# Small fp32 products of a mixer's branches: one by one between dense steps, or in runs

## The chip, the core and the metric

The kernel runs on one core of one Trainium2 chip. Its time is the device time of one launch in microseconds (us); of several runs the median is given. Five engines work in parallel, each through its own queue in order: TensorE (PE in the profile, its weight loads PEld), VectorE (DVE), ScalarE (ACT), GpSimd (POOL) and SyncE (SP), which issues most of the DMAs. They wait for each other through semaphores.

## The reference

One layer of a trunk on 512 tokens of width 1024: a mixer of four branches, cross attention to 256 memory tokens, and a gated feed-forward network with a convolution. Each is normed before and after, all in fp32. What matters here are three of the four branches:

```python
def gla_branch(q, k, v, r, a_lr, w_alpha, b_alpha, norm_g):      # chunks of 64 tokens, 4 heads of 64
    glog = jax.nn.log_sigmoid((a_lr @ w_alpha + b_alpha)) / GLA_TAU     # a_lr has 16 columns
    gcum = jnp.cumsum(heads(glog), axis=2)
    ...
    scores = jnp.where(causal, jnp.einsum('bnihd,bnjhd->bnhij', q_dec, k_dec), 0.0)
    o_intra = jnp.einsum('bnhij,bnjhv->bnihv', scores, vh)
    kv = jnp.einsum('bnjhd,bnjhv->bnhdv', k_to_end, vh)
    # a scan over the 8 chunks: state = exp(decay) * state + kv
    o = o_intra + jnp.einsum('bnihd,bnhdv->bnihv', q_dec, s_prev)
    o = o * lax.rsqrt(jnp.mean(o * o, axis=-1, keepdims=True) + EPS)
    return o * norm_g * jax.nn.silu(r)

def sgu_branch(u, v, ln_g, ln_b, w_s, b_s):                      # chunks of 128 tokens, 4 groups of 64
    vn = layer_norm(v, ln_g, ln_b)
    mixed = jnp.einsum('gij,bnjgc->bnigc', w_s * mask, vn) + b_s
    return u * mixed

def rglru_branch(xr, gate, ...):                                 # a linear recurrence over the tokens
    xc = causal_dwconv(xr, conv_w, conv_b)
    r, i = sigmoid(xc @ w_a + b_a), sigmoid(xc @ w_x + b_x)      # block-diagonal, 4 blocks of 64
    ...
```

## The kernel before

All activations are kept channel-major: a tile holds 128 channels by 512 tokens. The large products ("dense") are computed from fp32 values that are split into a high and a low part (type fp32r), as three products each: high by high, low by high and high by low (lines 125, 126 and 127, the function `mm3`). One such triple for one 128-row block of the contraction is a k-step, and `dense` makes eight of them for a contraction over 1024. The input projections (`w_in`, tile `win`) are eighteen dense products in a row, each with its own 128 output channels; then come the gates (tile `gate`) and the products of the branches with `w_branch` (tile `br`), 8 + 2 k-steps for each of 8 output blocks and 4 branches. Weights come by DMA into `raw`, ScalarE casts them to `whi` (line 75), and VectorE subtracts for `wlo` (line 76).

The branches' own small products are plain fp32, which TensorE does in two passes (two matmul rows in the profile for each). They are written as generators, called fibers. After each k-step `dense` calls `pump()`, which advances the first fiber to its next `yield`. So what a fiber issues between two yields stands between two k-steps of TensorE, up to what the tile framework's scheduler moves in ordering each engine's queue.

- `decay_fiber` issues the rank-16 product z (line 406, 16 rows of the array, four products), from which ScalarE and VectorE make the decays (tile `ee`, then `m`, `e`, `ep` and `dl`). `sgu_fiber` makes the layer norm (`vn`) and the token mixing `mx` (line 383, sixteen products, 64 columns of the array each, a pair on the two halves of the columns between two yields). Both run beside the first two projections, whose outputs are taken from PSUM by `kr` (line 352, VectorE).
- `gla_fiber(p)`, once for each half p of the heads, issues four transposes `ktT` (line 432, copied by ScalarE to `ktt`), eight score products `s` (line 442, 64 rows of the array each, first four on the one half hh of the rows, then four on the other), seven state products `kv` (line 457, 64 rows each, alternating halves), and for the output `o` eight products with 64 columns each (line 477) and seven on the whole array (line 482). VectorE masks the scores into `st` (line 446) and makes the running states `ss` (lines 468 and 470), two instructions per chunk. Then come a norm over heads (`hsum`, line 490, `rw`, `rbg`, line 501).
- `lru_fiber(p)` issues `gr` and `gi` (line 551, whole array).

PSUM has eight banks, which are allotted in turn: two with tag A (the outputs of the dense projections and gates), four with tag B (`ktT`, `s`, `kv`, `o`) and two with tag C (`z`, `mx`, `gr`, `gi`, `hsum`, `rbg`, `br`).

Of the kernel before, what the change touches and what calls it, by code (L numbers as in the profile page):

```python
# [16 lines left out]
P = 128  # L17
# [22 lines left out]
def tile_trunk(ctx: ExitStack, tc: tile.TileContext, a: dict, out: bass.AP):  # L40
# [114 lines left out]
            put(src)  # L155
        return hi, lo

# [1 line left out]
    par = cp.tile([P, NPAR], F32, name="par")  # L159

    def pc(name, i):
# [61 lines left out]
                              start=True, stop=True)  # L223
        return ps

# [1 line left out]
    x = [get(f"x{k}") for k in range(KT)]  # L227
    VA = 256 + 16
    vps = [bank("B", f"va{t}") for t in range(4)]
# [76 lines left out]
    def vtok(t, c0, c1):  # L306
        return vt[t // 2][:, (t % 2) * 256 + c0:(t % 2) * 256 + c1]

# [1 line left out]
    lngb = get("lngb")  # L310
    sync.dma_start(lngb[:, 0:256], a["ln_g"].partition_broadcast(P))
    sync.dma_start(lngb[:, 256:512], a["ln_b"].partition_broadcast(P))
# [30 lines left out]
    R2 = range(2)  # L343
# [8 lines left out]
        vector.tensor_tensor(t, ps, rb0s, op=ALU.mult)  # L352
        return t

# [1 line left out]
    mixed = []  # L356

    def sgu_fiber():
        vn = []
        for t in range(4):  # L360
            if t % 2 == 0:
                vnt = get("vn")
                vn.append(vnt)
            c = slice((t % 2) * 256, (t % 2 + 1) * 256)
            sv = svt[t // 2][:, c]
            st6 = tp.tile([P, 6], F32, tag="st6", name=f"st6_{t}")
            vector.bn_stats(st6, sv)
            mv = tp.tile([P, 2], F32, tag="mv", name=f"mv_{t}")
            vector.bn_aggr(mv, st6)
            sd = tp.tile([P, 1], F32, tag="sd", name=f"sd_{t}")  # L370
            scalar.activation(sd, mv[:, 1:2], AF.Sqrt, bias=epsc)
            vector.reciprocal(sd, sd)
            vector.tensor_scalar(vnt[:, c], sv, mv[:, 0:1], sd, op0=ALU.subtract, op1=ALU.mult)
            vector.tensor_mul(vnt[:, c], vnt[:, c], lngb[:, 0:256])
            vector.tensor_add(vnt[:, c], vnt[:, c], lngb[:, 256:512])
            yield
        put(*svt, lngb)
        for p in R2:
            mx = bank("C", "mx")
            for t in range(4):  # L380
                for j in R2:
                    g = 2 * p + j
                    tensor.matmul(mx[j * 64:(j + 1) * 64, t * P:(t + 1) * P],
                                  lhsT=vn[t // 2][:, (t % 2) * 256 + g * 64:(t % 2) * 256 + (g + 1) * 64],
                                  rhs=sguw[:, g * P:(g + 1) * P], start=True, stop=True)
                yield
            yc = get("yc")
            vector.tensor_tensor(yc.rearrange("p (n i) -> p n i", n=4), mx.rearrange("p (n i) -> p n i", n=4),
                                 sgub[:, p * P:(p + 1) * P].unsqueeze(1).to_broadcast([P, 4, P]), op=ALU.add)
            vector.tensor_mul(yc, yc, rb0s)  # L390
            mixed.append(yc)
        put(*vn, sguw, sgub)

# [1 line left out]
    gl_q = [get("ep") for _ in R2]  # L395
    gl_k = [get("e") for _ in R2]
    gl_kte = [get("m") for _ in R2]
# [3 lines left out]
    def decay_fiber():  # L401
        zs = [bank("C", "z") for _ in R2]
        for p in R2:
            for t in R2:
                tt = slice(t * 256, (t + 1) * 256)
                tensor.matmul(zs[p][:, tt], lhsT=walpha[:, p * P:(p + 1) * P], rhs=alr[0:16, tt],
                              start=True, stop=True)
                yield
        ee = wp.tile([P, 1024], F32, tag="raw", bufs=4, name="ee")
        for p in R2:  # L410
            scalar.activation(ee[:, p * S:(p + 1) * S], zs[p], AF.Abs, bias=pc("balpha", p))
            vector.tensor_scalar(gl_kte[p], zs[p], pc("balpha", p), 0.0, op0=ALU.add, op1=ALU.min)
        scalar.activation(ee, ee, AF.Exp, scale=-1.0)
        scalar.activation(ee, ee, AF.Ln, bias=1.0)
        for p in R2:
            vector.tensor_sub(gl_kte[p], gl_kte[p], ee[:, p * S:(p + 1) * S])
            vector.tensor_tensor_scan(gl_k[p], scanm, gl_kte[p], 0.0, op0=ALU.mult, op1=ALU.add)
        for p in R2:
            gc3 = gl_k[p].rearrange("p (n i) -> p n i", i=64)
            last = gc3[:, :, 63:64]  # L420
            vector.tensor_sub(gl_kte[p].rearrange("p (n i) -> p n i", i=64), last.to_broadcast([P, 8, 64]), gc3)
            scalar.activation(gl_dl[p].unsqueeze(2), last, AF.Exp, scale=1.0 / 16.0)
            scalar.activation(gl_q[p], gl_k[p], AF.Exp, scale=1.0 / 16.0)
            scalar.activation(gl_kte[p], gl_kte[p], AF.Exp, scale=1.0 / 16.0)
            scalar.activation(gl_k[p], gl_k[p], AF.Exp, scale=-1.0 / 16.0)
            vector.tensor_mul(gl_q[p], gl_q[p], rb0s)
        put(alr, scanm)

    def gla_fiber(p):
        kt_ps = bank("B", "ktT")  # L430
        for t in range(4):
            tensor.transpose(kt_ps[:, t * P:(t + 1) * P], gl_kte[p][:, t * P:(t + 1) * P], ident)
            yield
        ktt = get("ktt")
        scalar.copy(ktt, kt_ps)
        st = []
        for hh in R2:
            f = slice(hh * 64, hh * 64 + 64)
            s_ps = bank("B", "s")
            for t in range(4):  # L440
                tt = slice(t * P, (t + 1) * P)
                tensor.matmul(s_ps[:, tt], lhsT=gl_k[p][f, tt], rhs=gl_q[p][f, tt], start=True, stop=True)
                yield
            sm = get("st")
            gpsimd.memset(sm, 0.0)
            vector.copy_predicated(sm.rearrange("p (n i) -> p n i", n=4),
                                   causal.bitcast(I32).unsqueeze(1).to_broadcast([P, 4, P]),
                                   s_ps.rearrange("p (n i) -> p n i", n=4))
            st.append(sm)
        ss = [get("ss") for _ in R2]  # L450
        for t in ss:
            gpsimd.memset(t, 0.0)
        kv = [bank("B", "kv0"), bank("B", "kv1")]
        for n in range(7):
            r = slice((n % 2) * 64, (n % 2) * 64 + 64)
            c = slice((n // 2) * P, (n // 2 + 1) * P)
            tensor.matmul(kv[n % 2][:, c], lhsT=ktt[r, c], rhs=vtok(n // 2, p * P, (p + 1) * P)[r, :],
                          start=True, stop=True)
            yield
            for hh in R2:  # L460
                f = slice(hh * 64, hh * 64 + 64)

                def at(m):
                    return ss[m // 4][f, (m % 4) * P + hh * 64:(m % 4) * P + hh * 64 + 64]

                src = kv[n % 2][f, (n // 2) * P + hh * 64:(n // 2) * P + hh * 64 + 64]
                if n == 0:
                    vector.tensor_copy(at(1), src)
                else:
                    vector.scalar_tensor_tensor(at(n + 1), at(n), gl_dl[p][f, n:n + 1], src,  # L470
                                                op0=ALU.mult, op1=ALU.add)
        o_ps = bank("B", "o")
        for t in range(4):
            tt = slice(t * P, (t + 1) * P)
            for hh in R2:
                f = slice(hh * 64, hh * 64 + 64)
                tensor.matmul(o_ps[f, tt], lhsT=vtok(t, p * P + hh * 64, p * P + hh * 64 + 64),
                              rhs=st[hh][:, tt], start=True, stop=False)
            yield
            for n in (2 * t, 2 * t + 1):  # L480
                if n > 0:
                    tensor.matmul(o_ps[:, n * 64:(n + 1) * 64], lhsT=ss[n // 4][:, (n % 4) * P:(n % 4 + 1) * P],
                                  rhs=gl_q[p][:, n * 64:(n + 1) * 64], start=False, stop=n % 2 == 1)
            yield
        sq = get("sq")
        scalar.activation(sq, o_ps, AF.Square)
        yield
# [11 lines left out]
        for t in range(4):  # L499
            tt = slice(t * P, (t + 1) * P)  # L500
            tensor.matmul(rb[:, tt], lhsT=rw[:, tt], rhs=ident, start=True, stop=True)
            yield
        scalar.copy(sq, rb)
        vector.scalar_tensor_tensor(sq, o_ps, pc("glang", p), sq, op0=ALU.mult, op1=ALU.mult)
        put(*st, ktt, *ss, rw, gl_q[p], gl_k[p], gl_kte[p])
# [3 lines left out]
        put(gl_r[p])  # L509
        y[1][p] = split(sq, "yb", True)  # L510

# [1 line left out]
    lam = cp.tile([P, 2], F32, name="lam")  # L513
    la = [tp.tile([P, 2], F32, tag=f"la{i}", bufs=1, name=f"la{i}") for i in range(5)]
    pos8, neg8 = la[3], la[4]
# [27 lines left out]
    def lru_fiber(p, rx):  # L543
# [4 lines left out]
        for i, ps in enumerate((gr, gi)):  # L548
            for t in R2:
                tt = slice(t * 256, (t + 1) * 256)  # L550
                tensor.matmul(ps[:, tt], lhsT=lruw[:, i * 256 + p * P:i * 256 + (p + 1) * P], rhs=xc[:, tt],
                              start=True, stop=True)
                yield
        rr, ii = rx, get("ii")
        scalar.activation(rr, gr, AF.Sigmoid, bias=pc("lba", p))
        scalar.activation(ii, gi, AF.Sigmoid, bias=pc("lbx", p))
# [14 lines left out]
        put(rr)  # L571
        y[3][p] = split(gg, "yd", True)

# [1 line left out]
    fibers += [decay_fiber(), sgu_fiber()]  # L575
    for p in R2:
        kr = normed(w_in(), "kr")
# [41 lines left out]
        put(r)  # L619
        gl_r.append(sg)  # L620

# [1 line left out]
    acc = [None] * KT  # L623
    merged = []
    for ki, kb in enumerate(order):
# [23 lines left out]
        put(*t)  # L649
    put(rb0s, lruw, *vt)  # L650

# [1 line left out]
    mm = [get("mem") for _ in range(4)]  # L653
    for j in range(4):
        sync.dma_start(mm[j], a["memT"][j])
# [25 lines left out]
        if m == KT - 3:  # L681
            scalar.activation(warm, yg[m][:, tok][:, 0:1], AF.Sqrt, scale=0.0, bias=epsc)

# [1 line left out]
    yg, ssum = [], {}  # L685
    for m in range(KT):
        ps = bank("A", "mo")
# [30 lines left out]
            h2.append(split(hk, "h2", True))  # L718
        return h2

# [1 line left out]
    kk = [(get("kh", F32R), get("kl", F32R)) for _ in range(4)]  # L722
    for m in range(KT):
        ps = bank("A", "kT")
# [19 lines left out]
    for t in mem:  # L744
        put(*t)

# [1 line left out]
    def wq(hd):  # L748
        q = []
        for i in range(2):  # L750
# [127 lines left out]
    for c, ts in kept:  # L878
        put(*ts)

# [1 line left out]
    def up_post(j, ps):  # L882
        u = get("u")
        vector.tensor_tensor(u, ps, rb3, op=ALU.mult)
# [174 lines left out]
```

## Time and profile before

| what | value |
|---|---|
| three runs | 979.79, 980.82, 980.82 us, median 980.82 |
| profiled execution: span from its first to its last instruction | 978.7 us (its own launch time is not among the data; the median run is 2.1 us above this span) |
| TensorE busy, weight loads busy | 964.3 us, 802.6 us |
| VectorE busy, ScalarE busy | 574.7 us, 420.7 us |
| granted clock of TensorE, mean | 0.996 |
| first z to last rbg (the stretch of the small products) | 34 to 196 us |

The timeline gives the start of an instruction, its duration, engine, line, operation, tiles written and read, the shape, and how many alike were put together (x2). Matmuls are pipelined and the next starts before the last one's row ends, so what an instruction costs is read from the starts of what follows it. The groups by line give count, busy time and mean ns. A bracket at the end of a row is the idle time of that engine before it, and who ended it.

### The profile page before, as it was taken

How to read it: one execution, taken by the hardware profiler on the slowest of the kernel's cores; microseconds unless marked ns; L12 is line 12 of the kernel's file. 1: busy time of each engine (PE TensorE's matmuls, PEld its weight loads, DVE VectorE, ACT ScalarE, POOL GpSimd, SP SyncE). 2: the span in 40 equal slices, each digit the busy share in tenths (PEclk: the TensorE clock that was granted, in tenths of full speed). 3: DMA queues.
4: the chain of work that ended last, by engine and by line, in shares of the span. 5: the costliest groups of instructions: out<-in, count | busy, mean ns of one | idle time of the engine just before them, and what ended most of it. 6: DMA issues, size and time to landing. Idle time of an engine off the chain costs nothing.

```text
span 978.7 us, 12151 instructions
## 1 busy us (share of the span) xinstructions
PE 964.3 (99%) x4782; PEld 802.6 (82%) x4782; DVE 574.7 (59%) x886; ACT 420.7 (43%) x637; POOL 11.8 (1%) x33
## 2 busy tenths in 40 slices
PE   7999999999999999999999999999999999999996
PEld 7778687688888888889888889988888888888886
DVE  4776456445455565639865635897777777622314
ACT  7836136233223353545644554554444444322411
POOL 2000000000000000000000000000000000000001
PEclk9999999999999999999999999999999999999998
DMA  9342122132334333335431340132323232332302
GB/s 333 120 126 88 44 86 64 47 105 89 106 103 134 119 97 107 108 96 163 151 113 60 108 130 1 63 106 91 105 89 106 88 104 85 96 96 86 116 1 86
DMA packets 32648, 98.27 MB, mean 100 GB/s; under 512 B 4288, under 2 KB 7248, under 8 KB 32592
## 3 DMA queue, kind: packets, MB, share of 16 engines
q1 hardware_dynamic: 32416, 97.48, 31.4%
q8 instruction: 37, 0.61, 0.3%
q14 instruction: 19, 0.16, 0.1%
q0 software_dynamic: 32, 0.02, 0.0%
q10 hardware_dynamic: 144, 0.00, 0.0%
HBM read 95.39 MB, written 2.10 MB: 100 GB/s over the span
## 4 chain that ended last, share of the span: by engine, by line
PE 97%; issue 1%; ACT 1%; DVE 0%; DMA 0%; SPq 0%; DVEq 0%
PE up L126 8%; PE up L125 8%; PE up L127 8%; PE gate L125 6%; PE gate L127 6%; PE gate L126 6%; PE dn L127 4%; PE dn L125 4%; PE dn L126 4%; PE win L125 4%; PE win L127 3%; PE win L126 3%; PE br L125 2%; PE wo L127 2%; PE wo L125 2%; PE wo L126 2%
## 5 line engine op out<-in xcount | busy, mean ns | idle before, releaser
L75 ACT CAST whi<-raw 128x1024 fp32r<-128x1024 f32 x158 | 164.4, 1042 | 316.3 <-issue 146.0
L76 DVE TENSOR_TENSOR wlo<-raw,whi 128x1024 fp32r<-128x1024 f32 x158 | 191.1, 1211 | 129.9 <-ACT whi L75 128.5
L127 PE MATMUL up<-h3h,wlo 128*128 128x512 f32 (+1 forms) x368 | 138.2, 376 | 0.0
L126 PE MATMUL up<-h3l,whi 128*128 128x512 f32 (+1 forms) x368 | 138.1, 375 | 0.0
L125 PE MATMUL up<-h3h,whi 128*128 128x512 f32 (+1 forms) x368 | 138.1, 375 | 0.0
L125 PE MATMUL gate<-xgh,whi 128*128 128x512 f32 x256 | 101.9, 398 | 0.0
L127 PE MATMUL gate<-xgh,wlo 128*128 128x512 f32 x256 | 100.0, 390 | 0.0
L126 PE MATMUL gate<-xgl,whi 128*128 128x512 f32 x256 | 99.7, 389 | 0.0
L127 PEld LDWEIGHTS up<-h3h,wlo 128*128 128x128 f32 x368 | 69.3, 188 | 12.6
L125 PEld LDWEIGHTS up<-h3h,whi 128*128 128x128 f32 x368 | 69.3, 188 | 12.5
L126 PEld LDWEIGHTS up<-h3l,whi 128*128 128x128 f32 x368 | 69.3, 188 | 12.2
L352 DVE TENSOR_TENSOR sg<-gate,rb0s 128x512 f32<-128x512 f32 x32 | 22.1, 690 | 81.5 <-PE gate L127 81.5
L538 DVE SCALAR_TENSOR_TENSOR c<-u,par,c 128x511 f32<-128x511 f32 (+1 forms) x88 | 65.0, 746 | 1.3
L125 PE MATMUL win<-xgh,whi 128*128 128x512 f32 x144 | 61.0, 424 | 0.0
L125 PE MATMUL dn<-gh,whi 128*128 128x512 f32 x154 | 59.9, 389 | 0.0
L126 PE MATMUL dn<-gl,whi 128*128 128x512 f32 x154 | 59.9, 389 | 0.0
L127 PE MATMUL dn<-gh,wlo 128*128 128x512 f32 x154 | 59.9, 389 | 0.0
L125 PEld LDWEIGHTS gate<-xgh,whi 128*128 128x128 f32 x256 | 48.1, 188 | 11.4 <-issue 0.5
L127 PE MATMUL win<-xgh,wlo 128*128 128x512 f32 x144 | 56.6, 393 | 0.0
L127 PEld LDWEIGHTS gate<-xgh,wlo 128*128 128x128 f32 x256 | 48.1, 188 | 10.2
L126 PE MATMUL win<-xgl,whi 128*128 128x512 f32 x144 | 56.3, 391 | 0.0
L126 PEld LDWEIGHTS gate<-xgl,whi 128*128 128x128 f32 x256 | 48.1, 188 | 8.9
(348 smaller groups left out, 1752.5 us busy)
## 6 DMA issues: line engine op xcount, KB each, us to landing
raw<-in_w_up SPq DMA_DIRECT2D x44, 512.0 KB, 3.5
raw<-in_w_gate SPq DMA_DIRECT2D x32, 512.0 KB, 3.5
raw<-in_w_in SPq DMA_DIRECT2D x18, 512.0 KB, 3.5
raw<-in_w_down SPq DMA_DIRECT2D x16, 512.0 KB, 3.6
raw<-in_w_br SPq DMA_DIRECT2D x8, 512.0 KB, 3.4
raw<-in_w_mix SPq DMA_DIRECT2D x8, 512.0 KB, 3.5
raw<-in_w_k SPq DMA_DIRECT2D x8, 512.0 KB, 3.5
raw<-in_w_v SPq DMA_DIRECT2D x8, 512.0 KB, 3.5
```

Source lines behind the costliest of these rows:

```text
L75: scalar.copy(hi[:, :n], raw[:, :n])
L76: vector.tensor_tensor(lo[:, :n], raw[:, :n], hi[:, :n].bitcast(F32), op=ALU.subtract)
L125: tensor.matmul(ps, lhsT=w[0], rhs=x[0], start=first, stop=False)
L126: tensor.matmul(ps, lhsT=w[0], rhs=x[1], start=False, stop=False)
L127: tensor.matmul(ps, lhsT=w[1], rhs=x[0], start=False, stop=last)
L352: vector.tensor_tensor(t, ps, rb0s, op=ALU.mult)
L538: vector.scalar_tensor_tensor(dst[:, s:S], src[:, 0:S - s], pc(wname, (taps - 1 - s) * stride + off), dst[:, s:S], op0=ALU.mult, op1=ALU.add)
```

## The change

The yields are moved. z's four products, mx's sixteen, ktT's four with s's eight, kv's seven, o's fifteen, gr and gi's four and rbg's four are each issued between two k-steps. The eight products of s alternate between the halves of the rows, which write two banks. The state updates now come after all kv products, one chunk per yield. In front of mx and of kv the fiber passes three k-steps. In o only the first product on each half of the columns clears the bank (`start`), and the products with the states come after all others. The number of products, their operands and their shapes stay. Comments that fall away shift nothing; line numbers after the changed places move by a few (442 becomes 444, 457 becomes 463, 383 becomes 385).

```diff
@@ sgu_fiber
         put(*svt, lngb)
+        for _ in range(3):
+            yield
+        mxs = [bank("C", "mx") for _ in R2]
         for p in R2:
-            mx = bank("C", "mx")
             for t in range(4):
                 for j in R2:
                     g = 2 * p + j
-                    tensor.matmul(mx[j * 64:(j + 1) * 64, t * P:(t + 1) * P],
+                    tensor.matmul(mxs[p][j * 64:(j + 1) * 64, t * P:(t + 1) * P],
                                   ...
-                yield
+        yield
+        for p in R2:
+            mx = mxs[p]
             yc = get("yc")
...
@@ decay_fiber
                 tensor.matmul(zs[p][:, tt], lhsT=walpha[:, p * P:(p + 1) * P], rhs=alr[0:16, tt],
                               start=True, stop=True)
-                yield
+        yield
...
@@ gla_fiber
             tensor.transpose(kt_ps[:, t * P:(t + 1) * P], gl_kte[p][:, t * P:(t + 1) * P], ident)
-            yield
         ktt = get("ktt")
         scalar.copy(ktt, kt_ps)
+        sps2 = [bank("B", f"s{hh}") for hh in R2]
+        for t in range(4):
+            tt = slice(t * P, (t + 1) * P)
+            for hh in R2:
+                f = slice(hh * 64, hh * 64 + 64)
+                tensor.matmul(sps2[hh][:, tt], lhsT=gl_k[p][f, tt], rhs=gl_q[p][f, tt], start=True, stop=True)
+        yield
         st = []
         for hh in R2:
-            f = slice(hh * 64, hh * 64 + 64)
-            s_ps = bank("B", "s")
-            for t in range(4):
-                tt = slice(t * P, (t + 1) * P)
-                tensor.matmul(s_ps[:, tt], lhsT=gl_k[p][f, tt], rhs=gl_q[p][f, tt], start=True, stop=True)
-                yield
             sm = get("st")
             ...
+        for _ in range(3):
+            yield
         kv = [bank("B", "kv0"), bank("B", "kv1")]
         for n in range(7):
             ...
             tensor.matmul(kv[n % 2][:, c], lhsT=ktt[r, c], rhs=vtok(n // 2, p * P, (p + 1) * P)[r, :],
                           start=True, stop=True)
-            yield
+        yield
+        for n in range(7):
             for hh in R2:
                 ...
                     vector.scalar_tensor_tensor(at(n + 1), at(n), gl_dl[p][f, n:n + 1], src,
                                                 op0=ALU.mult, op1=ALU.add)
+            yield
         o_ps = bank("B", "o")
         for t in range(4):
             ...
                 tensor.matmul(o_ps[f, tt], lhsT=vtok(t, p * P + hh * 64, p * P + hh * 64 + 64),
-                              rhs=st[hh][:, tt], start=True, stop=False)
-            yield
-            for n in (2 * t, 2 * t + 1):
-                if n > 0:
-                    tensor.matmul(o_ps[:, n * 64:(n + 1) * 64], lhsT=ss[n // 4][:, (n % 4) * P:(n % 4 + 1) * P],
-                                  rhs=gl_q[p][:, n * 64:(n + 1) * 64], start=False, stop=n % 2 == 1)
-            yield
+                              rhs=st[hh][:, tt], start=t == 0, stop=False, skip_group_check=True)
+        for n in range(1, 8):
+            tensor.matmul(o_ps[:, n * 64:(n + 1) * 64], lhsT=ss[n // 4][:, (n % 4) * P:(n % 4 + 1) * P],
+                          rhs=gl_q[p][:, n * 64:(n + 1) * 64], start=False, stop=n == 7, skip_group_check=True)
+        yield
...
             tensor.matmul(rb[:, tt], lhsT=rw[:, tt], rhs=ident, start=True, stop=True)
-            yield
+        yield
...
@@ lru_fiber
                 tensor.matmul(ps[:, tt], lhsT=lruw[:, i * 256 + p * P:i * 256 + (p + 1) * P], rhs=xc[:, tt],
                               start=True, stop=True)
-                yield
+        yield
```

TensorE at the scores of the first half of the heads, beside the projection `win_973` (names carry the number of the tile; `xgh` and `xgl` are the parts of the activations). Before:

```order
L127 MATMUL win_973<-xgh_278,wlo_906 128x512
L442 MATMUL s_1010<-ep_514,e_516 128x128
L125 MATMUL win_973<-xgh_312,whi_905 128x512
L126 MATMUL win_973<-xgl_313,whi_905 128x512
L127 MATMUL win_973<-xgh_312,wlo_906 128x512
L442 MATMUL s_1010<-ep_514,e_516 128x128
L125 MATMUL win_973<-xgh_351,whi_905 128x512
```

After, where the two names `s_117_998` and `s_118_999` are the two banks:

```order
L127 MATMUL win_973<-xgh_140,wlo_906 128x512
L436 MATMUL ktT_991<-ident,m_518 128x128 x4
L444 MATMUL s_117_998<-ep_514,e_516 128x128
L444 MATMUL s_118_999<-ep_514,e_516 128x128
L444 MATMUL s_117_998<-ep_514,e_516 128x128
L444 MATMUL s_118_999<-ep_514,e_516 128x128
L444 MATMUL s_117_998<-ep_514,e_516 128x128
L444 MATMUL s_118_999<-ep_514,e_516 128x128
L444 MATMUL s_117_998<-ep_514,e_516 128x128
L444 MATMUL s_118_999<-ep_514,e_516 128x128
L125 MATMUL win_973<-xgh_171,whi_905 128x512
```

The products of the first head's half stood behind one k-step each; all eight now stand behind the transposes, without a k-step between them.

VectorE at the end of the second projection, whose bank `kr` empties (`yc` is the mixed tokens of the spatial gating). Before:

```order
L388 TENSOR_TENSOR yc_662<-mx_641,sgub_494 128x512
L352 TENSOR_TENSOR kr_678<-win_618,rb0s_394 128x512
L390 TENSOR_TENSOR yc_662<-yc_662,rb0s_394 128x512
L578 TENSOR_TENSOR m_519<-kr_678,m_519 128x512
L579 TENSOR_TENSOR e_517<-kr_678,e_517 128x512
```

After:

```order
L392 TENSOR_TENSOR yc_662<-mx_641,sgub_494 128x512
L392 TENSOR_TENSOR yc_665<-mx_642,sgub_494 128x512
L394 TENSOR_TENSOR yc_662<-yc_662,rb0s_394 128x512
L394 TENSOR_TENSOR yc_665<-yc_665,rb0s_394 128x512
L352 TENSOR_TENSOR kr_683<-win_628,rb0s_394 128x512
```

Three of the four `yc` instructions that stood behind `kr` or around it are now ahead of it.

VectorE at the states of the second half of the heads (`ydl` and `gg` belong to the recurrence, `sg` to the gates). Before:

```order
L153 TENSOR_TENSOR ydl_1405<-gg_1020,ydh_1404 128x512
L468 COPY ss_1500<-kv_183_1504 64x64 x2
L470 SCALAR_TENSOR_TENSOR ss_1500<-ss_1500,dl_521,kv_184_1505 64x64 x2
L470 SCALAR_TENSOR_TENSOR ss_1500<-ss_1500,dl_521,kv_183_1504 64x64 x2
L470 SCALAR_TENSOR_TENSOR ss_1501<-ss_1500,dl_521,kv_184_1505 64x64 x2
L470 SCALAR_TENSOR_TENSOR ss_1501<-ss_1501,dl_521,kv_183_1504 64x64 x2
```

After:

```order
L477 SCALAR_TENSOR_TENSOR ss_1428<-ss_1428,dl_521,kv_180_1460 64x64
L571 SCALAR_TENSOR_TENSOR rx_865<-av_1386,xc_1365 128x512
L477 SCALAR_TENSOR_TENSOR ss_1428<-ss_1428,dl_521,kv_180_1460 64x64
L576 TENSOR_TENSOR gg_1049<-gg_1049,rx_865 128x512
L477 SCALAR_TENSOR_TENSOR ss_1428<-ss_1428,dl_521,kv_179_1459 64x64 x2
L477 SCALAR_TENSOR_TENSOR ss_1429<-ss_1428,dl_521,kv_180_1460 64x64
L153 TENSOR_TENSOR ydl_1396<-gg_1049,ydh_1395 128x512
```

The states came behind the recurrence; they now stand among its scan (`rx`, line 571) and what follows it. On ScalarE in the same place, the copy `ktt` now stands ahead of the cast `whi` and of the sigmoid `sg` that it stood behind. The other engines' queues keep their instructions, and SyncE its DMAs.

More of the change, by code (lines that the diff above doesn't have):

```diff
@@ L447, in gla_fiber @@
                                    causal.bitcast(I32).unsqueeze(1).to_broadcast([P, 4, P]),
-                                   s_ps.rearrange("p (n i) -> p n i", n=4))
+                                   sps2[hh].rearrange("p (n i) -> p n i", n=4))
             st.append(sm)
```

## Prediction

> **What bounds the kernel now.** I read the page first: span, engines, granted clock, chain; then what TensorE waits for.
>
> ```profile
> span 978.7 us, 12151 instructions
> ...
> PE 964.3 (99%) x4782; PEld 802.6 (82%) x4782; DVE 574.7 (59%) x886; ACT 420.7 (43%) x637; POOL 11.8 (1%) x33
> ...
> PEclk9999999999999999999999999999999999999998
> ...
> PE 97%; issue 1%; ACT 1%; DVE 0%; DMA 0%; SPq 0%; DVEq 0%
> ```
> ```profile
> PE va L239 <- ACT xgh L253: 4.5, 1, 4.5
> ```
>
> The chain of waits is TensorE almost throughout, at a steady full clock, and its longest wait for another engine is 4.5 us in the first norm, before anything that changes. So whatever TensorE spends less between 34 and 196 us shortens the program, unless it then waits for someone. TensorE's busy share does not tell the cost of a small product, because matmuls overlap; the distance between the starts of dense steps does. That is read in the timeline of TensorE, an undisturbed step first, then steps with one small product behind them:
>
> ```profile
> 57.50 0.39 PE L125 MATMUL win<-xgh,whi 128*128 128x512 f32 x1
> ...
> 58.18 0.39 PE L125 MATMUL win<-xgh,whi 128*128 128x512 f32 x1
> ```
> ```profile
> 97.28 0.50 PE L125 MATMUL win<-xgh,whi 128*128 128x512 f32 x1
> ...
> 98.17 0.48 PE L442 MATMUL s<-ep,e 64*128 64x128 f32 x2
> 98.59 0.50 PE L125 MATMUL win<-xgh,whi 128*128 128x512 f32 x1
> ...
> 111.71 0.51 PE L125 MATMUL win<-xgh,whi 128*128 128x512 f32 x1
> ...
> 113.02 0.50 PE L125 MATMUL win<-xgh,whi 128*128 128x512 f32 x1
> ```
>
> A plain step lasts 58.18 - 57.50 = 0.68. With a score product s (98.59 - 97.28) or a state product kv (113.02 - 111.71) it lasts 1.31: each costs 0.63. What is product and what is excursion, full-array products in a run tell:
>
> ```profile
> 26.26 1.05 PE L221 MATMUL bctok<-ident,rs 128*128 128x128 f32 x8
> 27.07 0.36 PE L239 MATMUL sv<-svwh,xgh 128*128 128x256 f32 x1
> ```
>
> Eight passes (an fp32 product is two) of 128 moving columns take 0.81, so a pass takes 0.10 to 0.11 and a product 0.21. Of the 0.63, 0.42 goes into leaving the full array and coming back.
>
> **Part by part.** How many there are:
>
> ```profile
> L442 PE MATMUL s<-ep,e 64*128 64x128 f32 x32 | 7.8, 322 | 0.0
> L457 PE MATMUL kv<-vt,ktt 64*128 64x128 f32 x28 | 6.8, 322 | 0.0
> ```
>
> 32 and 28 passes are 16 and 14 products; 15 a fiber, 15 x 0.63 = 9.45. Now each fiber has one run of 8 and one of 7. What a run costs when two products use different halves of the array, the token mixing shows, whose pairs stand on two halves of the columns:
>
> ```profile
> 49.19 0.50 PE L125 MATMUL win<-xgh,whi 128*128 128x512 f32 x1
> ...
> 50.08 0.44 PE L383 MATMUL mx<-sguw,vn 128*64 128x128 f32 x4
> 50.45 0.50 PE L125 MATMUL win<-xgh,whi 128*128 128x512 f32 x1
> ...
> 51.34 0.66 PE L383 MATMUL mx<-sguw,vn 128*64 128x128 f32 x8
> 51.93 0.50 PE L125 MATMUL win<-xgh,whi 128*128 128x512 f32 x1
> ...
> 52.73 0.40 PE L125 MATMUL win<-xgh,whi 128*128 128x512 f32 x1
> ```
>
> One pair holds TensorE 0.37 (50.45 - 50.08), two pairs 0.59: the second pair adds 0.22, as much as one full-array product. So halves of the columns run side by side. Runs that alternate between halves of the rows are in no row of before. Bounds: 0.11 a product if row halves overlap as column halves do, 0.21 if not. I take 0.11, since the mx row is the nearest: two small tiles of the array beside each other, in a run. Then a run is 0.42 + 4 x 0.22 = 1.30, two are 2.6, a fiber saves 6.85 and both 13.7. Without overlap the runs are 2.10 and 1.89 and both fibers save 10.9.
>
> mx itself: a pair costs 50.45 - 49.19 - 0.68 = 0.58, the last two pairs 51.93 - 50.45 - 0.68 = 0.80; 6 x 0.58 + 0.80 = 4.28 before. All eight pairs in a run: 0.58 + 7 x 0.22 = 2.12. Saves 2.16.
>
> z, the decay's rank-16 product, is on one set of rows, so nothing alternates:
>
> ```profile
> 36.42 0.50 PE L125 MATMUL win<-xgh,whi 128*128 128x512 f32 x1
> ...
> 37.32 0.69 PE L406 MATMUL z<-alr,walpha 16*128 16x256 f32 x2
> 37.95 0.50 PE L125 MATMUL win<-xgh,whi 128*128 128x512 f32 x1
> ```
>
> 1.53 - 0.68 = 0.85 each, 3.40 for four; less 0.42 it is 0.43 of product. A run: 0.42 + 4 x 0.43 = 2.14. Saves 1.26. The Trainium skill ("TensorE: Matmul & The Clock Gate", Part 3, The mechanism) says that a weight load overlaps running matmuls only where the row group differs, and gives a load as columns / 1.2 ns; an estimate by that page adds 8 x 0.11 to the run and leaves 0.4 of the saving. The trace disagrees: bctok's passes, all on the same rows, follow at 0.10.
>
> o, from its first step to the first plain one after it:
>
> ```profile
> 115.65 0.50 PE L125 MATMUL win<-xgh,whi 128*128 128x512 f32 x1
> ...
> 119.10 0.50 PE L125 MATMUL win<-xgh,whi 128*128 128x512 f32 x1
> ...
> 119.90 0.55 PE L482 MATMUL o<-ep,ss 128*128 128x64 f32 x4
> 120.26 0.47 PE L125 MATMUL win<-xgh,whi 128*128 128x512 f32 x1
> ...
> 125.84 0.40 PE L125 MATMUL win<-xgh,whi 128*128 128x512 f32 x1
> ```
>
> 10.19 less nine steps of 0.68 is 4.07. After: eight products on column halves like four pairs of mx, 0.58 + 3 x 0.22 = 1.24, then seven on the full array; two in a step cost 1.16 - 0.68 = 0.48, five more add 0.22 each: 1.58. Saves 4.07 - 2.82 = 1.25 a fiber, 2.5 in all.
>
> The transposes ktT, the gates' gr and gi and the last rbg are full-array products: by bctok a run costs its passes, with no excursion to save. Taken at 0, bounds -0.3 and +0.3. Memsets, DMAs and weight loads are issued as before; no queue is passed by more than its place among steps.
>
> Sum on TensorE: 1.3 + 2.2 + 13.7 + 2.5 = 19.7.
>
> **What is late next.** TensorE gets ahead of VectorE, which does the same work. Three places:
>
> ```profile
> 46.16 1.29 DVE L416 TENSOR_TENSOR m<-m,ee 128x512 f32<-128x512 f32 x2 [0.49 <-ACT ee L414]
> ...
> 53.81 0.68 DVE L352 TENSOR_TENSOR kr<-win,rb0s 128x512 f32<-128x512 f32 x1
> 54.41 0.68 DVE L390 TENSOR_TENSOR yc<-yc,rb0s 128x512 f32<-128x512 f32 x1
> ```
>
> (1) The projections use two banks in turn; the fourth can start when kr has emptied the second's. Before, that was at 54.4 and the fourth started at 57.50 (quoted above): 3.1 of slack. After, TensorE is 1.26 + 2.16 = 3.4 earlier, at 54.1, while VectorE does two more products with rb0s and one more addition ahead of kr (the order), 0.60 each by the starts of the last two rows: 56.2. VectorE cannot start earlier than ScalarE's ee lets it (the wait of 0.49); that comes with z perhaps 0.4 earlier. A wait of 1.7 to 2.1 by this; I take 2.0. The bounds are 0, if VectorE runs those rows earlier, and 3.
>
> (2) In the second fiber the last state ss must be there for the last products of o.
>
> ```profile
> L470 DVE SCALAR_TENSOR_TENSOR ss<-ss,dl,kv x24: 263/280/289, 109.2 to 181.5; 64x64 f32<-64x64 f32 x24
> ```
> ```profile
> L76 DVE TENSOR_TENSOR wlo<-raw,whi 128x1024 fp32r<-128x1024 f32 x158 | 191.1, 1211 | 129.9 <-ACT whi L75 128.5
> ```
> ```profile
> 168.44 1.21 DVE L565 TENSOR_TENSOR_SCAN rx<-av,xc 128x512 f32<-128x512 f32 x1
> ```
>
> From the kv run's end TensorE needs 8 x 0.68 for steps, 1.0 for the column halves and 1.5 for the rest: 8.0. VectorE has 14 state updates (0.29 each: 4.1), a wlo (1.2), the recurrence's scan (1.2) and four of 0.60: 8.9. A wait of 0.9, bounds 0 and 2. The first fiber has fewer other rows there (two of 0.6, none of the scan) and waits for nothing.
>
> (3) kv waits for ScalarE's copy ktt:
>
> ```profile
> 153.56 0.59 PE L551 MATMUL gr<-xc,lruw 128*128 128x256 f32 x2
> ...
> 154.70 0.59 PE L551 MATMUL gr<-xc,lruw 128*128 128x256 f32 x2
> ```
> ```profile
> L75 ACT CAST whi<-raw 128x1024 fp32r<-128x1024 f32 x158 | 164.4, 1042 | 316.3 <-issue 146.0
> ```
> ```profile
> 162.70 0.58 ACT L435 COPY ktt<-ktT 128x512 f32<-128x512 f32 x1
> ```
>
> It ended 9.7 after gr began; kv now starts about 7.8 after it (gr and gi 4 x 0.43, by z's product of the same width, ktT four passes, 0.4, the s run 1.3, six steps 4.1, leaving and entering 0.2). In the new order a cast (1.0) and a sigmoid (half as long a row, 0.5) no longer stand ahead of ktt, and gr's second half follows its first at 0.43, not at 1.14, so 0.7 earlier: 7.5. Taken at 0.1, bounds 0 and 1.
>
> Waits: 2.0 + 0.9 + 0.1 = 3.0. Net 19.7 - 3.0 = 16.7. The profiled span 978.7 becomes 962.0; the runs' median, 980.82, stands 2.1 above the span, for what lies around it, so 964.1.
>
> **Rivals.**
> - Row halves do not overlap: 2.8 less saved, and the later s run gives VectorE 0.8 back in (2): 980.8 - 19.7 + 2.8 + 2.2 = 966.1. For it: no row shows row halves in a run. Against: column halves overlap. The Trainium skill (same page, Part 3, Measured speedup vs the span model) has four row tiles at 3.07 times one; an estimate by that, 1.54 for two halves, gives a time near 965.
> - VectorE is later than summed: the waits double, 967.1; or it is never late, 961.1. For the first: in these stretches it is the busiest after TensorE. Against: most waits there are its own, for TensorE.
> - Each change of row half drains the array as an excursion does. At 0.42 a change s and kv cost what they cost now, and z, mx and o less the waits still gain 3.0: 977.8. Slower only from 0.63 + 3.0 / 30 = 0.73 a product; with a drain at both ends, 0.21 + 0.84, the 30 products lose 12.6: 990.4. Against: the mx rows, where the change of column half drains nothing.
>
> **How the numbers follow.** Forecast 964.1, 60 in 100 (its own range 962 to 965.5); no overlap 17; VectorE later or on time 15; drains at each change 8, half of it beyond 0.73. A difference of 0.2% (2 us) is about what a measurement of this kernel can tell from no change. Faster 0.94, same 0.02, slower 0.04. The range goes from 960 (no waits, and 1 for what full-array runs may save) to 969.5 (no overlap, waits doubled).
>
> **What would show it.** Right: s and kv rows of 8 and 7 products in runs with 1.2 to 1.4 from their first start to the next dense one; mx 2.0, z 2.0; TensorE idle some 2 us near 54, released by VectorE's kr, and under 1 near the second o run. Wrong: runs of s of 2 us or more (no overlap) or of 5 (drains); VectorE rows that release TensorE at any other place; or a later stage, beyond 200 us, that is slower than before, where nothing changes.

## The result, and the profile after

The changed kernel takes 964.03 us (median of four runs, 963.55 to 964.48), the kernel before 980.31 beside it (979.37 to 980.82): 16.3 us less, ratio 0.9836 with a 95% interval from 0.9822 to 0.985. The forecast was 964.1.

The page of the profiled execution (964.2 us), the lines that answer to those of before:

```profile
span 960.8 us, 12143 instructions
...
PE 944.7 (98%) x4782; PEld 801.1 (83%) x4782; DVE 575.4 (60%) x886; ACT 420.8 (44%) x637; POOL 11.9 (1%) x33
...
PEclk9999999999999999999999999999999999999998
...
PE 93%; DVE 2%; ACT 2%; issue 2%; DMA 0%; DVEq 0%; ACTq 0%
```

TensorE has as many instructions as before and is busy 19.6 us less; the clock is the same. In the chain of work that ended last its share fell from 97 to 93%, and VectorE and ScalarE now hold 2% each: TensorE waits for them somewhere. The waits of TensorE say where (total, times, longest):

```profile
PE win L125 <- DVE la L535: 1.8, 1, 1.8
...
PE o L488 <- DVE ss L477: 0.6, 3, 0.2
```

What the runs cost is read from TensorE's timeline. The first pass of the step ahead of each run, the run, and the first passes of the two steps behind it:

```profile
31.97 0.40 PE L125 MATMUL win<-xgh,whi 128*128 128x512 f32 x1
...
32.76 1.99 PE L410 MATMUL z<-alr,walpha 16*128 16x256 f32 x8
34.68 0.50 PE L125 MATMUL win<-xgh,whi 128*128 128x512 f32 x1
...
35.48 0.39 PE L125 MATMUL win<-xgh,whi 128*128 128x512 f32 x1
...
40.25 0.39 PE L125 MATMUL win<-xgh,whi 128*128 128x512 f32 x1
...
41.02 1.97 PE L385 MATMUL mx<-sguw,vn 128*64 128x128 f32 x32
...
43.72 0.40 PE L125 MATMUL win<-xgh,whi 128*128 128x512 f32 x1
...
91.15 1.16 PE L444 MATMUL s<-ep,e 64*128 64x128 f32 x16
92.24 0.50 PE L125 MATMUL win<-xgh,whi 128*128 128x512 f32 x1
...
94.42 0.39 PE L125 MATMUL win<-xgh,whi 128*128 128x512 f32 x1
...
95.19 1.16 PE L463 MATMUL kv<-vt,ktt 64*128 64x128 f32 x14
96.27 0.50 PE L125 MATMUL win<-xgh,whi 128*128 128x512 f32 x1
...
97.08 0.39 PE L125 MATMUL win<-xgh,whi 128*128 128x512 f32 x1
...
101.17 0.39 PE L125 MATMUL win<-xgh,whi 128*128 128x512 f32 x1
...
105.33 0.39 PE L125 MATMUL win<-xgh,whi 128*128 128x512 f32 x1
```

The distance from the step ahead to the second step behind, less two plain steps (1.36), is the whole cost of a run. The second step is taken because the first one behind a run is itself 0.12 longer than a plain one (35.48 - 34.68 = 0.80 against 0.68).

| run | cost measured | forecast |
|---|---|---|
| z, 4 products | 35.48 - 31.97 - 1.36 = 2.15 | 2.14 |
| mx, 16 products | 43.72 - 40.25 - 1.36 = 2.11 | 2.12 |
| kv, 7 products | 97.08 - 94.42 - 1.36 = 1.30 | 1.30 |
| s, 8 products, from first start to the next dense pass | 92.24 - 91.15 = 1.09; kv by the same measure 96.27 - 95.19 = 1.08, so s costs 1.30 too | 1.30 |
| o, first fiber | 105.33 - 101.17 - 1.36 = 2.80 | 2.82 |

The sixteen passes of s take 1.09 together, less than 16 x 0.11 = 1.76 one after another: the halves of the rows overlap.

### The profile page after: what moved, and what is told of

The parts are those of the page before. It is cut to its first block, busy times and chain, and to the rows that moved or that the text cites. A ratio compares the mean times of both kernels' runs of the same rounds, so it can differ in the third digit from the quotient of the medians.

```text
span 960.8 us, 12143 instructions
## 1 busy us (share of the span) xinstructions
PE 944.7 (98%) x4782; PEld 801.1 (83%) x4782; DVE 575.4 (60%) x886; ACT 420.8 (44%) x637; POOL 11.9 (1%) x33
## 4 chain that ended last, share of the span: by engine, by line
PE 93%; DVE 2%; ACT 2%; issue 2%; DMA 0%; DVEq 0%; ACTq 0%
PE up L127 8%; PE up L126 8%; PE up L125 8%; PE gate L126 6%; PE gate L125 6%; PE gate L127 6%; PE dn L125 4%; PE dn L127 4%; PE dn L126 4%; PE win L125 3%; PE win L127 3%; PE win L126 3%; PE wo L125 2%; PE wo L127 2%; PE wo L126 2%
## 5 line engine op out<-in xcount | busy, mean ns | idle before, releaser
L125 PE MATMUL gate<-xgh,whi 128*128 128x512 f32 x256 | 99.8, 390 | 0.0
L125 PE MATMUL win<-xgh,whi 128*128 128x512 f32 x144 | 57.1, 397 | 1.8 <-DVE la L535 1.8
```

The costliest lines, as they stand in the source:

```text
L125: tensor.matmul(ps, lhsT=w[0], rhs=x[0], start=first, stop=False)
```

## Where the time came from, place by place

Three places of the program at which both traces show the same pass: the first of z, the first of the fourth projection, and gr of the second recurrence. Before, z began at 34.27:

```profile
34.27 0.48 PE L406 MATMUL z<-alr,walpha 16*128 16x256 f32 x1
```

The other two of before (57.50 and 153.56) stand in the prediction. After, z is the row at 32.76 above, and the others:

```profile
52.34 0.39 PE L127 MATMUL win<-xgh,wlo 128*128 128x512 f32 x1
54.49 0.47 PE L125 MATMUL win<-xgh,whi 128*128 128x512 f32 x1 [1.76 <-DVE la L535]
...
142.52 1.02 PE L557 MATMUL gr<-xc,lruw 128*128 128x256 f32 x4
```

| place | before | after | ahead by | gained since the place above | forecast |
|---|---|---|---|---|---|
| z | 34.27 | 32.76 | 1.51 | - | - |
| fourth projection | 57.50 | 54.49 | 3.01 | 1.50 | 1.26 + 2.16 - 2.0 = 1.42 |
| gr of the second recurrence | 153.56 | 142.52 | 11.04 | 8.03 | 6.85 + 1.25 = 8.1 |
| end of the span | 978.7 | 960.8 | 17.9 | 6.9 | 8.1 - 0.9 - 0.1 = 7.1 |

The 1.51 at z is not the change's: nothing differs ahead of it, and in the traces of this study z begins anywhere between 32.2 and 34.3, by what the first norm does (TensorE's wait for `svwh` there, for one, is 0.7 before and none after). From z on the changed kernel saves 17.9 - 1.5 = 16.4 (forecast 16.7). To see effects of 1 us, the experiments below are therefore also compared by the time from z to the end of the span, which leaves that scatter out. Each ratio is to runs of the kernel before that were made beside that version, with medians from 979.94 to 980.31:

| version | median, us | ratio to before, interval | span | first z | z to end |
|---|---|---|---|---|---|
| before | 980.31 | 1 | 978.7 | 34.3 | 944.4 |
| after | 964.03 | 0.9836, 0.9822 to 0.985 | 960.8 | 32.8 | 928.0 |
| z and mx alone | 978.11 | 0.9983, 0.9974 to 0.9993 | 975.2 | 32.2 | 943.0 |
| fibers of heads and recurrence alone | 965.17 | 0.9855, 0.984 to 0.987 | 963.3 | 33.8 | 929.5 |
| halves not alternating | 964.30 | 0.9843, 0.9828 to 0.9858 | 962.2 | 33.4 | 928.8 |
| pairs, no runs | 974.12 | 0.9945, 0.993 to 0.996 | 971.3 | 32.9 | 938.4 |
| kr first | 961.04 | 0.9807, 0.9794 to 0.982 | 958.7 | 32.7 | 926.0 |
| o later | 962.09 | 0.9815, 0.9801 to 0.9828 | 959.2 | 32.4 | 926.8 |
| both of these | 960.17 | 0.9797, 0.9783 to 0.981 | 958.9 | 34.1 | 924.8 |
| both, s and kv in one run | 959.84 | 0.9796, 0.9782 to 0.9809 | 957.6 | 33.3 | 924.3 |
| both, s in blocks | 959.88, one run | - | 958.1 | 33.2 | 924.9 |

## Experiments: the parts

**z and mx alone.** The kernel before with the new `decay_fiber` and `sgu_fiber`; `gla_fiber` and `lru_fiber` as they were.

> Only z and mx in runs; the attention branch as before. Theory (excursion 0.42 shared, then VectorE late with kr): TensorE saves 1.3 + 2.2 = 3.4 and then waits 1.8 to 2.0 for kr at the fourth projection: 980.3 - 1.5 = 978.8, a released wait of TensorE near 53 us. Rival (the wait comes from the attention's runs or from both together): no wait, 976.9.

Measured: 978.11, and 1.4 less from z on (944.4 - 943.0), the forecast's 1.42. The timeline shows the wait with the same size as in the whole change:

```profile
53.89 0.47 PE L125 MATMUL win<-xgh,whi 128*128 128x512 f32 x1 [1.75 <-DVE la L534]
```

So z and mx bring little because more than half of their 3.4 us goes into this wait, and the wait does not depend on the fibers behind it.

**The fibers of heads and recurrence alone.** The reverse: the new `gla_fiber` and `lru_fiber`, the old z and mx.

> Only the attention branch (ktT, s, kv, o, rbg) and the gates' gr and gi in runs; z and mx as before. Theory: 13.7 + 2.5 + ktT's share 0.1, less a wait of 0.6 for the last states: 980.3 - 15.5 = 964.8, no wait near 53 us. Rival (part of this gain needs z and mx earlier): above 966.

Measured: 965.17, from z on 14.9 less. The two parts add up: 1.4 + 14.9 = 16.3 against 16.4 for the whole. Its waits have the one for ss and none at the fourth projection.

## Experiments: what the row halves do

**Halves not alternating.** From the changed kernel; the number of runs and of products stays, only their order in a run changes.

```diff
-        for t in range(4):
-            tt = slice(t * P, (t + 1) * P)
-            for hh in R2:
-                f = slice(hh * 64, hh * 64 + 64)
+        for hh in R2:
+            f = slice(hh * 64, hh * 64 + 64)
+            for t in range(4):
+                tt = slice(t * P, (t + 1) * P)
                 tensor.matmul(sps2[hh][:, tt], ...)
...
-        for n in range(7):
+        for n in (0, 2, 4, 6, 1, 3, 5):
             ... tensor.matmul(kv[n % 2][:, c], ...)
```

> As the changed kernel, but s takes the four products of one row half and then the four of the other, and kv n = 0, 2, 4, 6 and then 1, 3, 5. Theory (row halves run side by side, 0.11 a pair of passes): s run 1.09 becomes 0.2 + 16 x 0.107 = 1.9, kv run 1.08 becomes 1.7; two fibers + 2.9, and the wait for the last states (0.6) goes: 964.0 + 2.3 = 966.3. Rival (the gain is the shared excursion alone, the order of halves is nothing): 964.0, runs of 1.1.

Measured: 964.30, the number of the rival that says the order of halves is nothing. The timeline says otherwise:

```profile
91.76 1.71 PE L444 MATMUL s<-ep,e 64*128 64x128 f32 x16
93.40 0.50 PE L125 MATMUL win<-xgh,whi 128*128 128x512 f32 x1
```

s takes 93.40 - 91.76 = 1.64 instead of 1.09, kv 97.76 - 96.35 = 1.41 instead of 1.08: 0.55 and 0.33 more, 0.88 a fiber. That is five passes of 0.11 for s and three for kv. It fits one picture: the second half starts five passes after the first, and both then run side by side (5 + 8 = 13 passes for s in place of 8; 5 + 6 = 11 for kv). The single passes of the trace show it: the first half's weight loads start every 0.11 us from 91.76 on, the second half's first at 92.31, while two loads of the first half are still to come. In TensorE's queue the four products of the first half do stand ahead of the four of the second, so this is not the scheduler's doing. So the order costs 2 x 0.88 = 1.76, less than the 16 passes that the theory reckoned with. And the second fiber's wait for ss shrinks by 0.9, since TensorE comes later to o (its run there costs 163.09 - 158.56 - 1.36 = 3.17 instead of the 4.05 worked out below; one idle time of 0.15 is left of three): 1.76 - 0.9 = 0.9, measured 0.8 from z to the end. The rival hit the time for a wrong reason: a gain lost and a wait given back, too small together for the medians to tell.

**Pairs, no runs.** The kernel before, with two products of s on the two halves of the rows between two k-steps, and the same for kv, instead of one.

```diff
+        sps2 = [bank("B", f"s{hh}") for hh in R2]
+        for t in range(4):
+            tt = slice(t * P, (t + 1) * P)
+            for hh in R2:
+                f = slice(hh * 64, hh * 64 + 64)
+                tensor.matmul(sps2[hh][:, tt], ...)
+            yield
...
         for n in range(7):
             ... tensor.matmul(kv[n % 2][:, c], ...)
-            yield
+            if n % 2 == 1 or n == 6:
+                yield
```

> The kernel before, with s and kv as pairs on the two row halves, one pair between two k-steps; all else as before. Theory: a pair costs 0.42 + 0.22 = 0.64, as one product did: s 4 x 0.64 against 8 x 0.63, kv 3 x 0.64 + 0.63 against 7 x 0.63, saves 4.3 a fiber: 980.3 - 8.7 = 971.6. Rival (halves do not overlap): a pair 0.85, saves 5.8: 974.5. Rival (alternating is what saves, runs are not needed): 966.6.

Measured: 974.12, near the number for "no overlap". But again the timeline speaks for the overlap:

```profile
95.87 0.50 PE L125 MATMUL win<-xgh,whi 128*128 128x512 f32 x1
...
96.76 0.49 PE L441 MATMUL s<-ep,e 64*128 64x128 f32 x4
97.18 0.50 PE L125 MATMUL win<-xgh,whi 128*128 128x512 f32 x1
...
102.72 0.49 PE L459 MATMUL kv<-vt,ktt 64*128 64x128 f32 x2
103.14 0.50 PE L125 MATMUL win<-xgh,whi 128*128 128x512 f32 x1
```

A step with a pair of s lasts 97.18 - 95.87 = 1.31, exactly what a step with one product lasted before. The second product, on the other half of the rows, is free. What failed is my edit: of the kv pairs only the first stayed one (the row shows x2, a single product, and a dense pass behind it; that is the scheduler's order). Each fiber has 4 + 6 = 10 excursions instead of the 4 + 4 reckoned with. 15 - 10 = 5 excursions less a fiber, 0.63 each, both fibers: 6.3, less a new wait of 0.2 for ss: 6.1. Measured from z on: 944.4 - 938.4 = 6.0.

**s in blocks.** From the version with both waits taken out (below): two products of one half, then two of the other.

```diff
-        for t in range(4):
-            tt = slice(t * P, (t + 1) * P)
-            for hh in R2:
+        for t, hh in ((0, 0), (1, 0), (0, 1), (1, 1), (2, 0), (3, 0), (2, 1), (3, 1)):
+                tt = slice(t * P, (t + 1) * P)
                 f = slice(hh * 64, hh * 64 + 64)
...
-        for n in range(7):
+        for n in (0, 2, 1, 3, 4, 6, 5):
```

> The version with both waits taken out; s in blocks of two products (four passes) of one half of the rows, then two of the other (h0 h0 h1 h1 h0 h0 h1 h1), kv likewise (0 2 | 1 3 | 4 6 | 5). Theory: TensorE starts a pass of the other half as soon as no more than three unstarted passes stand ahead of it, as where eight stood ahead and the other half began five passes late. Then the second half begins one pass late, and s takes 9 slots of 0.112: 1.20 us from its first start to the next dense pass (1.09 in strict alternation), kv still 1.08. Rival: only the very next pass is looked at, the halves overlap by one pass at each border: 16 - 3 = 13 slots, 1.64 us. Second rival: it looks much further, 1.09. In time: 960.4, 961.7, 960.2.

```profile
89.52 1.26 PE L444 MATMUL s<-ep,e 64*128 64x128 f32 x16
90.71 0.50 PE L125 MATMUL win<-xgh,whi 128*128 128x512 f32 x1
```

s takes 1.19 (forecast 1.20), kv 94.75 - 93.66 = 1.09 (1.08): blocks of four passes cost one pass in s and none in kv, blocks of eight cost five and three. The lengths are those of the theory, but not its detail: by single passes the second half starts 13 ns after the first here, and the lost pass falls at the change of blocks in the middle. How far TensorE looks ahead is therefore not settled; that it looks past a few passes of the other half is. The time, 959.88 from one run, tells none of the three forecasts from the others.

## Experiments: the two waits

**kr first.** From the changed kernel: the mixed tokens `yc` are made eight steps later, behind `kr` of the second projection.

```diff
@@ sgu_fiber, behind the sixteen products of mx
-        yield
+        for _ in range(9):
+            yield
         for p in R2:
             mx = mxs[p]
             yc = get("yc")
```

> As the changed kernel, but the spatial gating's fiber passes nine k-steps after its mx run, so that VectorE's kr of the second projection stands ahead of the yc instructions. Theory (the fourth projection waits for kr, which three yc instructions of 0.6 hold up): the wait of 1.8 goes, 964.0 - 1.8 = 962.2. Rival (VectorE is late by its whole work there, so the wait moves to the next projection): 964.0, a wait of 1 to 2 us a few us later.

Measured: 961.04, from z on 2.0 less than after. VectorE at this place, after and in this version, and TensorE's pass in this version:

```profile
51.26 1.28 DVE L392 TENSOR_TENSOR yc<-mx,sgub 128x512 f32<-128x512 f32 x2
52.46 1.28 DVE L394 TENSOR_TENSOR yc<-yc,rb0s 128x512 f32<-128x512 f32 x2
53.66 0.68 DVE L352 TENSOR_TENSOR kr<-win,rb0s 128x512 f32<-128x512 f32 x1
54.26 0.15 DVE L535 TENSOR_TENSOR la<-la,la 128x2 f32<-128x2 f32 x1
```
```profile
51.20 0.68 DVE L352 TENSOR_TENSOR kr<-win,rb0s 128x512 f32<-128x512 f32 x1
...
54.80 0.15 DVE L536 TENSOR_TENSOR la<-la,la 128x2 f32<-128x2 f32 x1
```
```profile
54.55 0.39 PE L125 MATMUL win<-xgh,whi 128*128 128x512 f32 x1
```

After, four `yc` (2.4 us) stood ahead of `kr`, and the fourth projection started just behind `kr` and the tiny `la`, which the profile names as releaser. Here `kr` runs at 51.20 and TensorE begins a plain step at 54.55, before `la` has even started at 54.80. So `kr` is what held the bank; `la` only ended last.

**o later.** From the changed kernel: two k-steps more ahead of the output products.

```diff
+        yield
+        yield
         o_ps = bank("B", "o")
```

> As the changed kernel, but with two more k-steps between the last state update and o. Theory (o's last products wait for VectorE's states, three waits of 0.19 on TensorE and the passes lost around them, 1.2 in all by the starts at 157.97 to 160.81 against 1.6 in the first fiber): 964.0 - 1.0 = 963.0. Rival (the later o delays ScalarE and VectorE behind it, and a later wait takes its place): 964.0 or more.

Measured: 962.09, from z on 1.2 less than after. The intervals of the two ratios overlap, so it is the trace that shows the gain. The second fiber's products with the states, after and in this version:

```profile
156.18 0.39 PE L125 MATMUL br<-ych,whi 128*128 128x512 f32 x1
...
160.56 0.43 PE L488 MATMUL o<-ep,ss 128*128 128x64 f32 x2 [0.19 <-DVE ss L477]
...
161.59 0.40 PE L125 MATMUL gate<-xgh,whi 128*128 128x512 f32 x1
```
```profile
158.97 1.77 PE L490 MATMUL o<-ep,ss 128*128 128x64 f32 x14
```

After, the run costs 161.59 - 156.18 - 1.36 = 4.05 where the first fiber's costs 2.80: the wait is 1.25. The profile's list has 0.6 for it, because it counts idle time up to the modelled end of a row, and a product that finds its operand starts 0.22 behind the last, long before that row's end. Here all fourteen passes stand in one row.

**Both.** The two edits together.

> Both of these: kr ahead of yc and o two k-steps later. Theory: 962.2 - 1.0 = 961.2, no wait of TensorE between 33 and 200 us. Rival: the waits move, 963 to 964.

```profile
PE va L239 <- ACT xgh L253: 4.6, 1, 4.6
PE sv L239 <- ACT svwh L267: 1.1, 1, 1.1
PE rb L971 <- DVE rs L968: 0.6, 1, 0.6
PE sumtok L961 <- ACT sq L944: 0.5, 1, 0.5
```

960.17, from z on 3.2 less than after: 1.92 + 1.25, the two waits. None stands in the list at the changed places (the sv of 1.1 lies ahead of z). The interval of its ratio, 0.9783 to 0.981, lies below that of the changed kernel, 0.9822 to 0.985: this version is faster than both kernels above.

**s and kv in one run.** On top of both: s goes down to kv, the masks behind them, o two steps later.

```diff
+        for _ in range(4):
+            yield
+        kv = [bank("B", "kv0"), bank("B", "kv1")]
         for t in range(4):
...
                 tensor.matmul(sps2[hh][:, tt], ...)
+        for n in range(7):
...
+            tensor.matmul(kv[n % 2][:, c], ...)
         yield
         st = []
...
-        for _ in range(3):
-            yield
-        kv = [bank("B", "kv0"), bank("B", "kv1")]
-        for n in range(7):
...
-            tensor.matmul(kv[n % 2][:, c], ...)
-        yield
...
-        yield
-        yield
+        for _ in range(4):
+            yield
         o_ps = bank("B", "o")
```

> The version with both waits taken out, and now the s and the kv products of a fiber in one run instead of two (the causal masks and the sum over kv behind it; o two steps later, so that it finds its operands). Theory: the 0.42 us is paid for each excursion of the array, whatever it holds, so one excursion less per fiber saves 0.42 x 2 = 0.84: 960.17 - 0.84 = 959.3; the run from its first start to the next dense pass is 1.09 + 8 passes of 0.112 = 1.98 us. Rival: the price hangs on the products, not on the excursion: 960.2, and a run of 2.2 us. Second rival: the masks now stand ahead of the sum over kv on VectorE (1.34 us in the trace) and the o products wait for it again: 960.5 to 961.5, with a wait of TensorE for ss.

```profile
92.54 1.16 PE L451 MATMUL s<-ep,e 64*128 64x128 f32 x16
...
94.52 0.50 PE L125 MATMUL win<-xgh,whi 128*128 128x512 f32 x1
```

The run takes 94.52 - 92.54 = 1.98 in the first fiber, the theory's number. By the steps around the run, it costs 95.33 - 91.77 - 1.36 = 2.20, where s and kv apart cost 2.60: one excursion less is worth 0.40, about the 0.42 of an excursion. In the second fiber the run takes 2.12 (147.18 to 149.30), 0.14 more. There ScalarE's copy `ktt`, from which kv loads its weights, is late:

```profile
147.59 0.58 ACT L439 COPY ktt<-ktT 128x512 f32<-128x512 f32 x1
```
```profile
148.21 0.96 PEld L455 LDWEIGHTS kv<-vt,ktt 64*128 64x128 f32 x14
```

The copy ends at 147.59 + 0.58 = 148.17, and kv's first weight load starts at 148.21. From the first s to the first kv it is 148.22 - 147.18 = 1.04, against 93.54 - 92.54 = 1.00 in the first fiber, where the copy had ended at 91.33; from the first kv to the dense pass it is 1.08 against 0.98. Together that is the 0.14. No run moved the copy, so the cause is read from these times alone. From z on 0.5 is gained (theory 0.84), no wait for ss came back, and the medians (959.84 against 960.17) cannot tell the two versions apart.

## Why the prediction was right

The mechanism was right, and its sum: from z on 16.4 was saved against 16.7. That the median, 964.03, meets 964.1 to a tenth is luck on top. The profiled span is 960.8 and not the 962.0 that was forecast, mostly because z began 1.51 earlier, and that run's time stands 964.2 - 960.8 = 3.4 above its span and not 2.1; the two differences cancel.

- **The model** (a product's passes, plus 0.42 for each excursion) carries the sum. The runs in the table above cost what was forecast within 0.02, and pairs (1.31 a step, as with one product) and one run instead of two (1.98) confirm it in versions that it was not made from.
- **Row halves overlap.** The value taken from column halves, 0.11 a product, is right; the rival without it (966.1) is out by the 1.09 of s. The Trainium skill ("TensorE: Matmul & The Clock Gate", Part 3, Measured speedup vs the span model) gives 3.07 for four row tiles, from which an estimate of 1.54 for two halves was made; the trace differs: sixteen passes take 1.09, of which the eight of one half alone, at 0.11, are 0.88 and the rest is the way back, so two halves are worth a factor of 2. What the forecast did not say is that this needs products of the other half close behind: all of one half first costs 0.88 a fiber.
- **z's run**, all on the same rows, costs 2.15 against 2.14 summed. The Trainium skill's rule (same page, Part 3, The mechanism), by which a weight load overlaps running matmuls only where the row group differs, would have put 8 x 0.11 = 0.88 on top, if it is taken without the background weight buffer that the same section allows a load to go to; the trace disagrees with the rule so taken.
- **Drains at each change of half** are excluded by the same rows of s and kv.
- **Wait (1)**, forecast 2.0, cost 54.49 - 52.34 - 0.23 = 1.92, at the place and by the holder that was named; shown by taking it away.
- **Wait (2)**, forecast 0.9, cost 1.25: the one term that was mis-sized, by 0.35. The sign that was named for it, under 1, holds in the profile's list (0.6) and not by the starts. From the kv run's end TensorE needed 8.0 as summed. VectorE's 8.9 was 9.2, from 151.28, where kv ended, to 160.50 (the last row):

```profile
153.62 0.69 DVE L570 TENSOR_TENSOR xc<-xc,ii 128x512 f32<-128x512 f32 x1
154.34 0.27 DVE L477 SCALAR_TENSOR_TENSOR ss<-ss,dl,kv 64x64 f32<-64x64 f32 x1
...
158.35 2.15 DVE L477 SCALAR_TENSOR_TENSOR ss<-ss,dl,kv 64x64 f32<-64x64 f32 x7
```

  The forecast's 0.60 was the distance of two large rows in a stream, the rows of `yc` and `kr` in the prediction, where the next starts 0.08 before the row of 0.68 has ended. Here `xc`, `gg` and `ydl` run to their end first: 153.62 + 0.69 = 154.31, the next row at 154.34, and from `xc` to it 0.72. The scan does so too (from 154.54 to the next row at 155.78, 1.24 instead of 1.2). The fourth large row, `sg` ahead of the copies, keeps the 0.60 (152.52 to 153.12), so a small row behind a large one is not by itself what costs. I priced a chain by the pace of a stream; what holds the next row back in the chain no run tests.
- **Wait (3)**, forecast 0.1 for the second fiber, is not there. The first fiber's kv starts 0.09 after the end of the step ahead (94.42 + 0.68 = 95.10, and 95.19), for the entry. The second's starts just so: the step begins at 149.42, and kv at 150.19 = 149.42 + 0.68 + 0.09. The copy `ktt` had ended at 149.33 + 0.57 = 149.90.
- **gr, gi, ktT and rbg**, taken at 0 within 0.3, leave at most the few tenths by which the stretches of the table miss the sums.

## What to carry to other kernels

Where small products interrupt dense ones, price the excursion apart from the product: take the distance of two dense starts across it, less a plain step, less the product's own passes. Gather the products so that there are few excursions, and alternate the halves of the array within a gathering. Then ask who fed the engine that is now early: both new waits came from the order of another engine's queue and went away by moving a few `yield`s, for 3.2 us more from z to the end.

## What the runs showed of the hardware

- A product on one half of the rows beside one on the other half costs nothing more (1.31 a step with one or with two), weight loads included.
- TensorE starts products of the other half ahead of some that stand before them in its queue, so its queue is not kept in strict order: with eight passes of one half first, the second half came five passes late, not eight.
- Full-array fp32 products cost no excursion. After the change, gr and gi, eight passes of 256 columns, cost 144.94 - 141.84 - 1.36 = 1.74 by the steps around them, where four products of z, as wide, were reckoned at 4 x 0.43 = 1.72 without their excursion. The four transposes ktT, alone between two steps in the version with s and kv in one run, cost 90.38 - 88.56 - 1.36 = 0.46, four passes of 0.11:

```profile
88.56 0.39 PE L125 MATMUL win<-xgh,whi 128*128 128x512 f32 x1
...
89.24 0.60 PE L437 MATMUL ktT<-ident,m 128*128 128x128 f32 x4
...
90.38 0.40 PE L125 MATMUL win<-xgh,whi 128*128 128x512 f32 x1
```
